# Half of the second MLP product of a decoder layer by seven block products for eight, its sums kept in SBUF

## The chip, the core and the metric

The kernel runs on one core of one Trainium2 chip. The metric is the device time of one execution in microseconds; three executions are shown. The engines of the core are TensorE (PE in the profile, with PEld for its weight loads), VectorE (DVE), ScalarE (ACT), GpSimd (POOL) and SyncE (SP). Each has a queue of its own, which it works off in order; waits between engines are semaphores.

## What is computed

One layer of a decoder on 256 tokens (16 meta tokens are put ahead of them), width 2048: a token-mixing half, then an MLP. The change lies in the MLP and the norm around it:

```python
h_res = h_res + merged @ w_out[l]
h2 = rms_norm(h_res, norm_mlp_g[l])
h_res = h_res + jnp.square(jax.nn.relu(h2 @ w_mlp_in[l])) @ w_mlp_out[l]
...
y = rms_norm(h_res, final_norm_g)
return y[:, N_META:N_META + S]
```

`w_mlp_in` is 2048 x 8192 and `w_mlp_out` 8192 x 2048, in float32. By the end of the token mixing the meta tokens have done their work, so the MLP has 256 token rows.

## The kernel before

**Numbers.** Every float32 operand is split into a high part that TensorE reads in one pass (fp32r) and a low rest. A product is three matmuls: high by high, high by low, low by high.

**The stream.** All weights go through one list of `blocks`. SP loads a unit of 1 MB into one of three `raw` buffers; a unit has two blocks of 128 x 1024 elements. `convert(i)` splits a block: ACT casts `raw` to `hi` (L228), DVE subtracts to get `lo` (L233). `hi` and `lo` have four buffers each, so ACT can start on block j only when PE has ended block j-4. The loop at L1123 does, for each block i: `convert(i + 3)`, then at most one small job from the `side` queue, then the block's matmuls. This text order is the order of every engine's queue.

**The MLP** (`mlp_group`, L919) goes through the 8192 hidden columns in four groups of 2048. In a group, four slabs of the first product (`slab_t`, L269, eight blocks each, 16 matmul pairs of 512 and 256 columns per unit) make 16 hidden chunks `hid` of 128 columns x 256 tokens. After a slab's last block a `wave` (L130) takes four PSUM banks out: per bank ACT copies one half, DVE adds the other, DVE squares the positive part (L932), ACT casts and DVE subtracts. Then four slabs of the second product (`slab_n`, L304), of 512 output columns each, use `hid` as stationary: a block is two chunks x two token halves x three matmuls (L319, L320, L321) = 12 matmuls of 128x512. After 16 chunks DVE adds each of the two banks to the residual, `hr += r2sq * ps` (L949). `r2sq` is the square of the norm's factor, which is taken out of the squared ReLU. The last slab of the last group is `slab_last`, whose two token halves end one after the other, with `final` behind each.

PSUM has eight banks: five of a pool `g` and three of a pool `m`. The MLP uses only `g`: four for a `slab_t`, two for a `slab_n`. GpSimd has nothing to do in the MLP.

Of the kernel before, what the change touches and what calls it, by code (L numbers as in the profile page):

```python
# [8 lines left out]
F32 = mybir.dt.float32  # L9
# [41 lines left out]
POOL_FROM, POOL_TO = 20, 112  # L51


class Slots:
    def __init__(self, pool, n, dtype, name):
        self.free = deque(pool.tile([P, 2, L], dtype, name=f"{name}{i}") for i in range(n))
        self.low = n
# [16 lines left out]
def decoder_layer(ctx, tc, x, meta, g_mix, w_in, kv_g, ik_g, w_uk, w_uv, w_ao, w_pool,  # L74
# [9 lines left out]
    ptp = ctx.enter_context(tc.tile_pool(name="ptp", bufs=2))  # L84
    evp = ctx.enter_context(tc.tile_pool(name="evp", bufs=1))
    stp = ctx.enter_context(tc.tile_pool(name="stp", bufs=4))
    pg = ctx.enter_context(tc.tile_pool(name="pg", bufs=5, space=PSUM))
# [4 lines left out]
    plain = Slots(act, NPLAIN, F32, "f")  # L92
# [49 lines left out]
    ident = cst.tile([P, P], F32, name="ident")  # L142
    dup = cst.tile([IDIM, P], F32, name="dup")
    ones = cst.tile([P, P], F32, name="ones")
# [13 lines left out]
    grow = cst.tile([KC, P], F32, name="grow")  # L158
    A.dma_start(out=grow, in_=gain_rows(g_mix))
    grow2 = cst.tile([27, P], F32, name="grow2")  # L160
# [14 lines left out]
    class Block:  # L175
        def __init__(self, unit, src, shape, mm, pops=1, pre=None):
            self.unit, self.src, self.shape, self.mm, self.pops, self.pre = unit, src, shape, mm, pops, pre
            self.split_late = self.keep = False

# [27 lines left out]
    def split_block(b, i):  # L207
# [9 lines left out]
        else:  # L217
# [16 lines left out]
            b.hi, b.lo = hv, lv  # L234

# [33 lines left out]
    def slab_t(w, c0, tiles, rhs, nk=KC, done=None, wide=None, lead=False):  # L269
        """Output tiles [128 columns of w, tokens]; weights stationary."""  # L270
# [3 lines left out]
        def mm(k):  # L274
            def go(hi, lo):
# [18 lines left out]
                if k + 2 == nk:  # L294
                    wave([done(j, pss[j]) for j in range(tiles)])
# [8 lines left out]
    def slab_n(w, k_base, c0, lhs, nk, done):  # L304
        """Output tiles [128 tokens, 512 columns of w]; activations stationary."""
# [26 lines left out]
    def slab_last(w, k_base, c0, lhs, nk, done):  # L332
        """As slab_n, but the second half of the tokens follows the first on the same, kept weights."""
# [109 lines left out]
    bias = cst.tile([P, SC], F32, name="bias")  # L443
# [422 lines left out]

    def reload_x():
        for s in range(4):
# [12 lines left out]
    def mean_sq(t=slice(0, 2)):  # L881
        V.tensor_reduce(ssum[:, t], ss[:, t], axis=AX.X, op=ALU.add)
        V.tensor_scalar(ssum[:, t], ssum[:, t], 1.0 / D, EPS, op0=ALU.mult, op1=ALU.add)
# [26 lines left out]

    def norm2_stat():
        mean_sq()
        V.reciprocal(r2sq, ssum)

# [1 line left out]
    def rhs_h2(k):  # L916
        return h2[k], 0

    def mlp_group(gi):  # L919
        hid = []  # L920

        def done_1(s):
            def go(j, ps):
                t = slots.get()
                hid.append(t)
                u, st = pair(ps)
# [7 lines left out]
            return go  # L934
# [4 lines left out]
        def done_2(s):  # L939
            def go(t, ps):  # L940
                f = flat(hr[t][s])[:, 0:512]

                def last():
                    if s == 3 and t == 1:
                        for m in hid:
                            slots.put(m)
                    if gi == 3:
                        push(lambda: final_pre(t, s))
                return [lambda: V.scalar_tensor_tensor(out=f, in0=ps, scalar=r2sq[:, t:t + 1], in1=f,  # L949
                                                       op0=ALU.mult, op1=ALU.add), last]  # L950
            return go

        for s in range(4):
            slab_t(w1, gi * D + s * 512, 4, rhs_h2, done=done_1(s))
# [8 lines left out]
    def load_gf():  # L963
# [5 lines left out]
        A.activation(rstd, ssum, AF.Sqrt)  # L969

    def final_pre(t, s):
        square_piece(t, s)
        f = flat(hr[t][s])[:, 0:512]
        V.tensor_tensor(out=f, in0=f, in1=flat(gf[s])[:, 0:512], op=ALU.mult)

    def final(t, ps):
        f = flat(hr[t][3])
# [189 lines left out]
```

## Time and profile before

| | us |
|---|---|
| three executions | 1422.92, 1422.93, 1424.09 |
| their median | 1422.93 |
| profiled execution, first to last instruction (its span) | 1421.2 |
| median less span | 1.7 |

The profile is of one execution. The page gives no other time for the profiled one than its span; the 1.7 us are start and end outside the first and last instruction. Busy times by engine within the span: PE 1409.1 us in 7748 matmuls, DVE 856.4, ACT 696.2, GpSimd 188.7. [...]

### The profile page before, as it was taken

Reading aid. Unit: us, or ns where it says so; the run is one execution under the profiler, and the core shown is the slowest. Engines: PE = TensorE matmul, PEld = TensorE weight load, DVE = VectorE, ACT = ScalarE, POOL = GpSimd, SP = SyncE. Lnnn points to the kernel's source line nnn. Section 1 sums busy time; section 2 is a strip of 40 time slices with the busy share of each in tenths; the row PEclk is TensorE's granted clock in tenths of the full one; section 3 lists DMA queues with packets and bytes.
Section 4 is the critical chain, followed back from the end, with each engine's and each line's share of the span. In section 5 each row is a group of like instructions: output and inputs, shape, how many; then the busy total and the mean of one; then the engine's idle time right before and its main releaser. Section 6 shows DMA issues by size and latency. Waiting matters only on the chain.

```text
span 1421.2 us, 19595 instructions
## 1 busy us (share of the span) xinstructions
PE 1409.1 (99%) x7748; PEld 1212.0 (85%) x7748; DVE 856.4 (60%) x1279; ACT 696.2 (49%) x1070; POOL 188.7 (13%) x145
## 2 busy tenths in 40 slices
PE   9999999999999999999999999999999999999997
PEld 8888888899988888888888888888888888888886
DVE  5667965565567767665566545566455654556654
ACT  5655465555555745444544433454334443445452
POOL 1155454454304000000000000000000000000000
PEclk9999999999999999999999999999999999999999
DMA  6654454434546565665555556555555555565552
GB/s 226 202 171 147 163 162 155 153 118 140 162 156 201 178 199 202 210 220 187 183 178 185 200 178 196 189 179 196 188 188 195 180 181 202 180 188 193 183 192 104
DMA packets 135723, 256.21 MB, mean 180 GB/s; under 512 B 4710, under 2 KB 16016, under 8 KB 135632
## 3 DMA queue, kind: packets, MB, share of 16 engines
q1 hardware_dynamic: 134352, 251.68, 53.2%
q0 software_dynamic: 1248, 3.29, 0.8%
q8 instruction: 60, 0.98, 0.3%
q14 instruction: 31, 0.25, 0.1%
q10 hardware_dynamic: 32, 0.01, 0.0%
HBM read 252.86 MB, written 2.10 MB: 179 GB/s over the span
## 4 chain that ended last, share of the span: by engine, by line
PE 94%; DVE 4%; ACT 1%; issue 0%; DMA 0%; POOL 0%; DVEq 0%; POOLq 0%; ACTq 0%
PE g L292 34%; PE g L293 17%; PE g L319 10%; PE g L321 10%; PE g L320 10%; PE g L137 2%; PE g L139 2%; PE g L138 2%; PE m L137 1%; DVE lo L231 1%; PE m L138 1%; PE m L139 1%; PE g L343 1%; PE g L341 1%; PE g L342 1%; DVE f L544 1%
## 5 line engine op out<-in xcount | busy, mean ns | idle before, releaser
L292 PE MATMUL g<-r,hi 128*128 128x512 f32 x2240 | 793.7, 396 | 1.0 <-DVE f L124 1.0
L228 ACT CAST hi<-raw 128x1024 fp32r<-128x1024 f32 (+1 forms) x469 | 486.8, 1046 | 566.2 <-PE g L292 269.5
L233 DVE TENSOR_TENSOR lo<-raw,hi 128x1024 fp32r<-128x1024 f32 (+1 forms) x377 | 457.7, 1224 | 410.2 <-ACT hi L228 409.4
L293 PE MATMUL g<-r,lo 128*128 128x256 f32 x2240 | 630.6, 282 | 0.0
L292 PEld LDWEIGHTS g<-r,hi 128*128 128x128 f32 x2240 | 420.8, 188 | 99.4 <-DVE f L124 2.1
L293 PEld LDWEIGHTS g<-r,lo 128*128 128x128 f32 x2240 | 423.2, 189 | 0.2
L319 PE MATMUL g<-hi,r 128*128 128x512 f32 x608 | 241.6, 397 | 0.0
L321 PE MATMUL g<-hi,r 128*128 128x512 f32 x608 | 238.7, 393 | 0.0
L320 PE MATMUL g<-lo,r 128*128 128x512 f32 x608 | 238.4, 392 | 0.0
L231 POOL TENSOR_TENSOR lo<-raw,hi 128x512 fp32r<-128x512 f32 x92 | 154.8, 1689 | 212.9 <-ACT hi L228 212.2
L321 PEld LDWEIGHTS g<-hi,r 128*128 128x128 f32 x608 | 114.1, 188 | 27.9
L231 DVE TENSOR_TENSOR lo<-raw,hi 128x512 fp32r<-128x512 f32 x92 | 83.1, 904 | 89.6 <-ACT hi L228 89.6
L320 PEld LDWEIGHTS g<-lo,r 128*128 128x128 f32 x608 | 114.2, 188 | 25.6
L319 PEld LDWEIGHTS g<-hi,r 128*128 128x128 f32 x608 | 114.1, 188 | 25.4
L123 ACT COPY b<-g 128x256 f32<-128x256 f32 x148 | 54.7, 371 | 25.0 <-PE g L293 21.2
L115 ACT CAST r<-t 128x256 fp32r<-128x256 f32 x100 | 40.7, 407 | 44.0 <-DVE t L932 27.7
L137 PE MATMUL g<-r,hi 128*128 128x272 f32 (+1 forms) x192 | 56.9, 297 | 0.0
L139 PE MATMUL g<-r,lo 128*128 128x272 f32 (+1 forms) x192 | 55.8, 291 | 0.0
L138 PE MATMUL g<-r,hi 128*128 128x272 f32 (+1 forms) x192 | 55.7, 290 | 0.0
L124 DVE TENSOR_TENSOR t<-g,b 128x256 f32<-128x256 f32 x116 | 48.0, 417 | 0.2 <-ACT b L123 0.2
L116 DVE TENSOR_TENSOR r<-t,r 128x256 fp32r<-128x256 f32 x100 | 42.8, 428 | 4.3 <-ACT r L115 0.2
L137 PEld LDWEIGHTS g<-r,hi 128*128 128x128 f32 x192 | 36.5, 190 | 0.8
(190 smaller groups left out, 921.0 us busy)
## 6 DMA issues: line engine op xcount, KB each, us to landing
raw<-in_w_mlp_in_dram SPq DMA_DIRECT2D x64, 1024.0 KB, 5.3
raw<-in_w_mlp_out_dram SPq DMA_DIRECT2D x64, 1024.0 KB, 5.1
raw<-in_w_in_dram SPq DMA_DIRECT2D x56, 1024.0 KB, 5.0
raw<-in_w_attn_o_dram SPq DMA_DIRECT2D x16, 1024.0 KB, 5.1
raw<-in_w_out_dram SPq DMA_DIRECT2D x16, 1024.0 KB, 5.1
raw<-in_w_pool_o_dram SPq DMA_DIRECT2D x8, 1024.0 KB, 5.1
raw<-in_w_in_dram SPq DMA_DIRECT2D x8, 512.0 KB, 7.9
raw<-in_w_in_dram SPq DMA_DIRECT2D x4, 768.0 KB, 5.1
```

Of the source, the lines that this page charges most:

```text
L123: return t, [lambda: A.copy(b, ps[:, 1]), lambda: V.tensor_tensor(out=t, in0=ps[:, 0], in1=b, op=ALU.add)]
L137: T.matmul(ps, wh, xh, start=first, stop=False)
L138: T.matmul(ps, wh, xl, start=False, stop=False)
L139: T.matmul(ps, wl, xh, start=False, stop=last)
L228: A.copy(hv, src)
L231: e.tensor_tensor(out=lv[:, kk], in0=src[:, kk], in1=hv.bitcast(F32)[:, kk], op=ALU.subtract)
L233: V.tensor_tensor(out=lv, in0=src, in1=hv.bitcast(F32), op=ALU.subtract)
L292: T.matmul(ps, wh, xt[:, :, o:o + S], start=f, stop=False)
L293: T.matmul(ps[:, 0], wl, xt[:, 0, o:o + S], start=False, stop=l)
L319: T.matmul(ps, xh, hi[:, kk], start=f, stop=False)
L320: T.matmul(ps, xh, lo[:, kk], start=False, stop=False)
L321: T.matmul(ps, xl, hi[:, kk], start=False, stop=l)
```

## The change

The second product of a group is now walked 1024 output columns at a time (`mix_group`, two walks n = 0 and 1 in groups 0 to 2, one in group 3). A walk has eight units; a unit p holds hidden chunks 2p and 2p+1 by 1024 columns, that is a 2 x 2 grid of weight pieces, against a 2 x 2 grid of hidden pieces (two chunks by two token halves). Units 0, 2, 4, 7 are done plainly: two blocks of 12 matmuls, eight products in all. Units 1, 3, 5, 6 (`SUMS`) are done by a scheme of seven products, in three blocks a, b, c of 6, 6 and 9 matmuls. Its operands are sums: of hidden pieces (`combs`, made once per group and unit in the waves of the first product) and of weight pieces (`sums_a`, `sums_b`, made on DVE for each unit before the blocks are split). Block c splits one more piece of 512 columns (`extra`).

The products of all units go into eight banks, all of PSUM: four of them (11, 12, 21, 22) take what belongs to one quarter of the output (128 tokens x 512 columns), the other four (1, 5, 6, 7) what several quarters share. At the end of a walk each bank is copied out by ACT (`drain`) into one of a few temporaries and added to a running sum in SBUF by a DMA with an add, issued by GpSimd (in group 0 the shared banks' sums are just begun by the copy). The running sums of the quarters are the residual itself, which is divided by `r2sq` first (`scale_up`) and multiplied by it at the end (`final_pre`, `final`). In the last walk of each column half the banks are added by DVE from PSUM (`f1`, `f2`, `out`), and the shared running sums are joined into the quarters by eight DVE adds out of the side queue (`join`). The second column half of group 3 stays with `slab_n` and `slab_last`. Some constants and buffers of the early stages now lie in pools that are closed before the MLP, so that its new tiles fit.

```diff
+NWORK = 20
+SUMS = (1, 3, 5, 6)
+WALK = ((0, 1, 2, 3, 4, 5, 6, 7), (1, 0, 3, 2, 5, 4, 6, 7))
...
+    def scale_up(t, s):
...
+        A.activation(flat(r)[:, 0:512], flat(r)[:, 0:512], AF.Copy, scale=msq[:, t:t + 1])
...
+        def sums_a():
...
+            V.tensor_tensor(out=two(tt["a"]), in0=two(raw[:, 512:1536]),
+                            in1=raw[:, 0:512].unsqueeze(1).to_broadcast([P, 2, 512]), op=ALU.add)
+
+        def sums_b():
...
+            V.tensor_tensor(out=tt["b"][:, 0:512], in0=tt["a"][:, 0:512], in1=raw[:, 1024:1536], op=ALU.add)
+            V.tensor_tensor(out=tt["b"][:, 512:1024], in0=tt["b"][:, 0:512], in1=raw[:, 1536:2048], op=ALU.add)
+
+        def extra():
...
+            A.copy(bc.hi2, raw[:, 1536:2048])
+            V.tensor_tensor(out=bc.lo2, in0=raw[:, 1536:2048], in1=bc.hi2.bitcast(F32), op=ALU.subtract)
...
+        def c_mm(p, kk, x):
+            def go(hi, lo):
+                for c in ("22", "21", "12", "11"):
+                    t, h = CROSS[c]
+                    mm_n(bank[c], *a(2 * p + kk, t), hi[:, h], lo[:, h], kk == 0 and x == (first_c if c == "22" else 0), x == 7 and kk == 1)
...
+            def go_a(hi, lo):
+                mm_n(bank["5"], *cb(1), hi[:, 0], lo[:, 0], fr, la)
+                mm_n(bank["7"], *cb(0), hi[:, 1], lo[:, 1], fr, la)
+
+            def go_b(hi, lo):
+                mm_n(bank["6"], *cb(2), hi[:, 0], lo[:, 0], fr, la)
+                mm_n(bank["21"], *a(kb, 1), hi[:, 1], lo[:, 1], x == 0, False)
+
+            def go_c(hi, lo):
+                mm_n(bank["1"], *a(ka, 0), hi[:, 0], lo[:, 0], fr, la)
+                mm_n(bank["12"], *cb(3), hi[:, 1], lo[:, 1], x == 0, False)
+                mm_n(bank["11"], *a(kb, 0), own[0].hi2, own[0].lo2, x == 0, False)
...
+        def drain(c):
+            first = gi == 0 and c not in CROSS
+            r = plain.get()
+            if first:
+                acc[n, c] = r
+            A.copy(flat(r)[:, 0:512], bank[c])
+            if not first:
+                d = flat(acc[n, c])[:, 0:512]
+                G.dma_start(out=d, in_=flat(r)[:, 0:512], accum_op=ALU.add)
+                plain.put(r)
...
+        if not final:
+            for i, c in ((ls + 2, "5"), (ls + 2, "7"), (ls + 3, "6"), (ls + 4, "1"), (e, "22"), (e, "21"),
+                         (e, "12"), (e, "11")):
+                at(i, drain, c)
...
+                return [lambda: None, lambda: None,
+                        lambda: tt(out=c4[:, 0:2], in0=u4[:, 1:2].to_broadcast([P, 2, P]), in1=u4[:, 0:4:3],
+                                   op=ALU.subtract),
+                        lambda: tt(out=c4[:, 2], in0=u4[:, 0], in1=c4[:, 1], op=ALU.subtract),
+                        lambda: tt(out=c4[:, 3], in0=u4[:, 2], in1=c4[:, 2], op=ALU.subtract)] + \
+                    split_stages(comb[p][0], cs[:, 0:S], S) + split_stages(comb[p][1], cs[:, S:2 * S], S)
...
-        for s in range(4):
-            if gi < 3 or s < 3:
-                slab_n(w2, gi * KC, s * 512, lhs_hid, KC, done_2(s))
-            else:
-                slab_last(w2, gi * KC, s * 512, lhs_hid, KC, final)
...
+        for n in range(2 if gi < 3 else 1):
+            mix_group(gi, n, hid, comb, bank)
+        at(len(blocks), free)
+        if gi == 3:
+            slab_n(w2, gi * KC, 1024, lhs_hid, KC, done_2(2))
+            slab_last(w2, gi * KC, 1536, lhs_hid, KC, final)
...
+        for fn in hooks.pop(i, ()):
+            fn()
+        if i + 4 < len(blocks) and blocks[i + 4].sums is not None:
+            blocks[i + 4].sums()
```

**Where it moves instructions.** DVE, from the end of the last wave of the first product into the second, in group 0. `lo` are the splits, `t` and `r` a hidden chunk before and after its split. Before:

```order
L932 SCALAR_TENSOR_TENSOR t<-t 128x256
L116 TENSOR_TENSOR r_98<-t,r_98 128x256
L116 TENSOR_TENSOR r_99<-t,r_99 128x256
L233 TENSOR_TENSOR lo<-raw,hi 128x1024 x8
L949 SCALAR_TENSOR_TENSOR f_135<-g,r2sq,f_135 128x512
```

Now (`cs` are sums of hidden pieces, `ta` and `tb` sums of weight pieces, `xl` the extra piece's low part):

```order
L1162 SCALAR_TENSOR_TENSOR t<-t 128x256
L123 TENSOR_TENSOR r_129<-t,r_129 128x256
L1173 TENSOR_TENSOR cs<-us 128x256
L123 TENSOR_TENSOR r_108<-t,r_108 128x256
L1175 TENSOR_TENSOR cs<-us,cs 128x128
L1176 TENSOR_TENSOR cs<-us,cs 128x128
L123 TENSOR_TENSOR r_109<-cs,r_109 128x256
L123 TENSOR_TENSOR r_116<-cs,r_116 128x256
L241 TENSOR_TENSOR lo<-tb,hi 128x1024
L241 TENSOR_TENSOR lo<-raw,hi 128x1024
L1000 TENSOR_TENSOR xl<-raw,xh 128x512
```

Five operations more stand between the wave and the first split behind it, and that split is now the one for block b of unit 1.

DVE further on, in the middle of the walk, units 4 to 6 (before, eight splits in a row and then two L949 stand here):

```order
L986 TENSOR_TENSOR ta<-raw 128x1024
L241 TENSOR_TENSOR lo<-raw,hi 128x1024
L992 TENSOR_TENSOR tb<-ta,raw 128x512
L993 TENSOR_TENSOR tb<-tb,raw 128x512
L241 TENSOR_TENSOR lo<-ta,hi 128x1024
L241 TENSOR_TENSOR lo<-tb,hi 128x1024
L986 TENSOR_TENSOR ta<-raw 128x1024
L241 TENSOR_TENSOR lo<-raw,hi 128x1024
L1000 TENSOR_TENSOR xl<-raw,xh 128x512
L992 TENSOR_TENSOR tb<-ta,raw 128x512
L993 TENSOR_TENSOR tb<-tb,raw 128x512
L241 TENSOR_TENSOR lo<-ta,hi 128x1024
```

The sums stand among the splits, one block ahead of the split that needs them.

ACT, from the last units of walk 0 into walk 1 (before, only casts `hi` stand here); `g` and `m` are the banks, `w` the temporaries and running sums:

```order
L1064 COPY w_6271<-g 128x512
L236 CAST hi<-ta 128x1024
L1064 COPY w_6272<-g 128x512
L236 CAST hi<-tb 128x1024
L1064 COPY w_6273<-g 128x512
L236 CAST hi<-raw 128x1024
L999 CAST xh<-raw 128x512
L1064 COPY w_6262<-g 128x512
L1064 COPY w_6263<-m 128x512
L1064 COPY w_6264<-m 128x512
L1064 COPY w_6265<-m 128x512
L236 CAST hi<-raw 128x1024 x2
```

The copies out of the banks stand among the casts of the next walk's first blocks; from group 1 on the four temporaries serve both for the first four copies and for the last four.

## Rows read from the trace of the kernel before

**Rows 1.** Page, parts 1 and 2: busy us by engine, then granted clock in tenths.
```profile
PE 1409.1 (99%) x7748; PEld 1212.0 (85%) x7748; DVE 856.4 (60%) x1279; ACT 696.2 (49%) x1070; POOL 188.7 (13%) x145
...
PEclk9999999999999999999999999999999999999999
```
**Rows 2.** Page, part 4: shares of the chain that ended last, by engine.
```profile
PE 94%; DVE 4%; ACT 1%; issue 0%; DMA 0%; POOL 0%; DVEq 0%; POOLq 0%; ACTq 0%
```
**Rows 3.** Waits, whole span: who waited for whom, us in total, times, longest.
```profile
PE g L292 <- DVE f L124: 1.0, 2, 0.5
...
DVE lo L233 <- ACT hi L228: 409.4, 311, 2.7
```
**Rows 4.** Page, part 5, second product: count, busy us, mean ns, idle before.
```profile
L319 PE MATMUL g<-hi,r 128*128 128x512 f32 x608 | 241.6, 397 | 0.0
```
**Rows 5.** Timeline of PE in a `slab_n`: start us, us, instruction.
```profile
979.88 0.39 PE L319 MATMUL g<-hi,r 128*128 128x512 f32 x1
980.11 0.39 PE L320 MATMUL g<-lo,r 128*128 128x512 f32 x1
...
983.34 0.39 PE L319 MATMUL g<-hi,r 128*128 128x512 f32 x1
```
**Rows 6.** Timeline of ACT in the same slab: casts of successive blocks, idle before.
```profile
975.22 1.05 ACT L228 CAST hi<-raw 128x1024 fp32r<-128x1024 f32 x1 [1.72 <-PE g L321]
977.99 1.05 ACT L228 CAST hi<-raw 128x1024 fp32r<-128x1024 f32 x1 [1.73 <-PE g L321]
```
**Rows 7.** Timeline of DVE: a single split, and six subtractions of 512 in a row.
```profile
1001.27 1.23 DVE L233 TENSOR_TENSOR lo<-raw,hi 128x1024 fp32r<-128x1024 f32 x1 [1.55 <-ACT hi L228]
...
1382.46 3.70 DVE L216 TENSOR_TENSOR r<-raw,r 128x512 fp32r<-128x512 f32 x6
```
**Rows 8.** Timeline of DVE, wave at the end of a first-product slab.
```profile
898.72 0.42 DVE L124 TENSOR_TENSOR t<-g,b 128x256 f32<-128x256 f32 x1
...
901.98 0.42 DVE L932 SCALAR_TENSOR_TENSOR t<-t 128x256 f32<-128x256 f32 x1
902.31 0.98 DVE L116 TENSOR_TENSOR r<-t,r 128x256 fp32r<-128x256 f32 x2
903.83 3.50 DVE L233 TENSOR_TENSOR lo<-raw,hi 128x1024 fp32r<-128x1024 f32 x3 [0.53 <-ACT hi L228]
```
**Rows 9.** Timeline of ACT, the same wave.
```profile
896.50 1.05 ACT L228 CAST hi<-raw 128x1024 fp32r<-128x1024 f32 x1 [1.75 <-PE g L292]
...
902.43 0.41 ACT L115 CAST r<-t 128x256 fp32r<-128x256 f32 x1 [0.59 <-DVE t L932]
902.75 2.00 ACT L228 CAST hi<-raw 128x1024 fp32r<-128x1024 f32 x2
904.94 1.06 ACT L228 CAST hi<-raw 128x1024 fp32r<-128x1024 f32 x1 [0.20 <-PE g L292]
```
**Rows 10.** Groups by line and shape: ACT operations of 512 columns.
```profile
L215 ACT CAST r<-raw 128x512 fp32r<-128x512 f32 x8 | 4.3, 616 | 0.0
```
**Rows 11.** DMA issues of the span: count, KB each, median us from issue to landing.
```profile
raw<-in_w_mlp_out_dram SPq DMA_DIRECT2D x64, 1024.0 KB, 5.1
...
f<-in_x_dram POOLq DMA_DIRECT2D x8, 256.0 KB, 3.5
...
f<-in_final_norm_g_dram POOLq DMA_DIRECT2D x4, 256.0 KB, 4.7
```
**Rows 12.** Line L871, GpSimd's loads of x: time to issue, time to landing.
```profile
L871 POOL DMA_DIRECT2D f<-in_x_dram x8: 538/538/585, 449.5 to 563.0; - x8
...
DMA to landing us min/median/max: 3.4/3.5/4.1
```
**Rows 13.** Groups by line and shape: DVE subtractions of 512, beside GpSimd's and alone.
```profile
L231 DVE TENSOR_TENSOR lo<-raw,hi 128x512 fp32r<-128x512 f32 x92 | 83.1, 904 | 89.6 <-ACT hi L228 89.6
...
L216 DVE TENSOR_TENSOR r<-raw,r 128x512 fp32r<-128x512 f32 x8 | 5.0, 686 | 0.0
```

More of the change, by code (lines that the diff above doesn't have):

```diff
@@ L1 @@
-from collections import deque
+from contextlib import ExitStack
+from collections import defaultdict, deque
 import concourse.bass as bass
@@ L91, in decoder_layer @@
     slots = Slots(act, NSLOT, F32R, "r")
-    plain = Slots(act, NPLAIN, F32, "f")
+    plain = Slots(fpl, NPLAIN, F32, "f")
     V, A, T, G = nc.vector, nc.scalar, nc.tensor, nc.gpsimd
@@ L178, in __init__ @@
             self.split_late = self.keep = False
+            self.sums = self.extra = None
     def add_unit(load, halves):
@@ L234, in split_block @@
             b.hi, b.lo = hv, lv
+            if b.extra is not None:
+                b.extra()
     side = deque()
@@ L294, in go @@
                 if k + 2 == nk:
-                    wave([done(j, pss[j]) for j in range(tiles)])
+                    jobs = [done(j, pss[j]) for j in range(tiles)]
+                    wave(jobs + (more() if more else []))
             return go
@@ L865, in decoder_layer @@
     h2 = [None] * KC
+    late = {}
     def reload_x():
+        nonlocal plain
+        early.close()
+        late["pool"] = ctx.enter_context(tc.tile_pool(name="late", bufs=1, reuse_waits="tile"))
+        plain = Slots(late["pool"], NWORK, F32, "w", S)
         for s in range(4):
@@ L916, in rhs_h2, with at, mm_n, sums_tile @@
     def rhs_h2(k):
         return h2[k], 0
+    hooks = defaultdict(list)
+    acc = {}
+    hc = hr
+    CROSS = {"11": (0, 1), "12": (0, 0), "21": (1, 1), "22": (1, 0)}
+    def at(i, fn, *args):
+        hooks[i].append(lambda: fn(*args))
+    def mm_n(ps, xh, xl, wh, wl, first, last):
+        T.matmul(ps, xh, wh, start=first, stop=False)
+        T.matmul(ps, xh, wl, start=False, stop=False)
+        T.matmul(ps, xl, wh, start=False, stop=last)
+    def sums_tile(tag):
+        return late["pool"].tile([P, 1024], F32, tag=tag, name=tag)
@@ new lines, in join, with v, done @@
+    def join(n):
+        def v(c):
+            return flat(acc[n, c])[:, 0:512]
+        for d, c, op in (("6", "1", ALU.subtract), ("7", "6", ALU.add), ("6", "5", ALU.add), ("5", "7", ALU.add),
+                         ("12", "6", ALU.add), ("21", "7", ALU.subtract), ("22", "5", ALU.add), ("11", "1", ALU.add)):
+            push(lambda d=d, c=c, op=op: V.tensor_tensor(out=v(d), in0=v(d), in1=v(c), op=op))
+        def done():
+            for c in ("6", "7", "5", "1"):
+                plain.put(acc.pop((n, c)))
+        push(done)
@@ L919, in mlp_group, with stages @@
     def mlp_group(gi):
         hid = []
+        comb = {}
+        us = {}
         def done_1(s):
-            def go(j, ps):
+            sp = [p for p in (2 * s, 2 * s + 1) if p in SUMS]
+            def stages(j, ps):
+                c = 4 * s + j
                 t = slots.get()
                 hid.append(t)
-                u, st = pair(ps)
+                dst = None
+                if c // 2 in sp:
+                    if c % 2 == 0:
+                        us[c // 2] = late["pool"].tile([P, 512], F32, tag="us", name="us")
+                    dst = us[c // 2][:, (c % 2) * S:(c % 2 + 1) * S]
+                u, st = pair(ps, dst)
@@ L940, in go, with free @@
             def go(t, ps):
[L941 to L950, printed above, removed]
-            return go
+                f = flat(hc[t][s])[:, 0:512]
+                return [lambda: V.tensor_tensor(out=f, in0=ps, in1=f, op=ALU.add),
+                        lambda: push(lambda: final_pre(t, s))]
+            return go
+        if gi in (2, 3):
+            at(len(blocks) + 3, join, 3 - gi)
         for s in range(4):
-            slab_t(w1, gi * D + s * 512, 4, rhs_h2, done=done_1(s))
-        for s in range(4):
-            if gi < 3 or s < 3:
-                slab_n(w2, gi * KC, s * 512, lhs_hid, KC, done_2(s))
-            else:
-                slab_last(w2, gi * KC, s * 512, lhs_hid, KC, final)
+            done, more = done_1(s)
+            slab_t(w1, gi * D + s * 512, 4, rhs_h2, done=done, more=more)
+        bank = {}
+        def free():
+            for m in [m for v in comb.values() for m in v] + (hid if gi < 3 else []):
+                slots.put(m)
+        for n in range(2 if gi < 3 else 1):
+            mix_group(gi, n, hid, comb, bank)
+        at(len(blocks), free)
+        if gi == 3:
+            slab_n(w2, gi * KC, 1024, lhs_hid, KC, done_2(2))
+            slab_last(w2, gi * KC, 1536, lhs_hid, KC, final)
     gf = []
```

172 lines of the change are left out of this document (143 added, 29 removed).

## The prediction

> **What bounds the kernel now.** The page's first part, the shares of the chain and the list of waits come first. PE is busy for 99% of the span at the full granted clock [rows 1], the chain that ended last is PE for 94% of it [rows 2], and PE waits almost nowhere: its longest entry for a matmul of the first product is 1.0 us in all, while DVE spends 409 us waiting for ACT's casts, which in turn wait for PE to free a buffer [rows 3]. So the time is PE's work, and time comes off if there are fewer matmuls and nobody else becomes late.
>
> What is one matmul worth? The list of costly groups gives 397 ns as its mean [rows 4], but the rows overlap. The timeline has two L319 fifteen starts apart at 979.88 and 983.34, so 3.46 / 15 = 0.231 us each; ACT's casts, each released by the end of a block of 12, come 2.77 us apart, again 0.231 [rows 5, 6]. I price by the pace. The Trainium skill (Trainium Kernel Development and Optimization, Performance Expectations) says the same against the busy rows: matmul busy time is a bad metric because matmuls are pipelined. By the row's length the 84 matmuls below would be worth 33 us; by the pace, which the trace shows, 19.4.
>
> **What goes on PE.** A walk replaces two `slab_n` of 96 matmuls by four plain units of 24 and four summed units of 21, 180 in all. Seven walks take away 7 x 12 = 84 matmuls of 128x512; each takes its own weight load with it. 84 x 0.231 = **19.4 us**.
>
> **What it adds on DVE, the engine to watch.** A split of 1024 costs 1.23 us alone, but three in a row take 3.50, so 1.167 each where DVE is pressed; six subtractions of 512 take 3.70, 0.617 each [rows 7, 8]. A plain unit is two splits, 2.33 us of DVE against 24 x 0.231 = 5.55 of PE. A summed unit is sum a (1.167), two sums b (1.234), three splits (3.50) and the extra piece (0.617): 6.52 us of DVE against 21 x 0.231 = 4.86 of PE. So DVE loses 1.7 us in each summed unit and gains it back in the plain ones: a walk is 35.4 us of DVE against 41.6 of PE. No row shows an add with a broadcast source; I price it as the subtraction of the same size.
>
> The tight place is walk 0, where DVE starts late. Call S the end of PE's last block of the first product; in the trace S is 899.3 (the cast at 904.94 starts at the end of a block, two blocks of 2.83 earlier is S) [rows 9]. The wave now ends at S + 4.0 (902.31 + 0.98) [rows 8]. Five DVE operations (256, 128, 128, 256, 256 columns, about 0.33 and 0.25 each by the spacing of the wave, 901.98 to 902.31) and two ACT casts of 0.41 come behind it in a chain, so ACT casts block b of unit 1 from about S + 4.9, and DVE splits it from S + 6.0 to 7.2. PE has 5.55 of unit 0 and 1.39 of block a until then, 6.94: late by **0.2 us, in each of four groups, 0.8 us**. From S + 6.0 DVE has no pause: rest of unit 1 three operations, 2.95 us, unit 2 2.33, unit 3 6.52, unit 4 2.33, unit 5 6.52, and block a of unit 6 with its sums 3.57. That is 24.2 us, so this split ends at S + 30.2. PE needs it after units 0 to 5, at 3 x 5.55 + 3 x 4.86 + 0.2 = S + 31.4. Slack 1.2 us, the smallest of the walk; without it DVE's lag would go to PE one for one. In walk 1 no two summed units are neighbours and DVE enters it with an empty queue: no wait.
>
> **ACT.** A walk adds four times 1.05 + 0.62 for the third block and the extra piece, and eight copies of a bank at about 0.6 (512 columns from SBUF take 0.616) [rows 10]: 23.4 + 4.8 = 28 of 41.6 us. Not full. What matters is what is queued behind a copy: the casts of the next blocks. In walk 0 of groups 1 and 2 the last copy (bank 11) goes into the temporary from which bank 1's DMA is still adding. By the order above bank 1's copy follows the cast of the next walk's block b: DVE goes on from S + 30.2 with the rest of unit 6, unit 7 and that block's sums, to S + 37.9, then the cast 1.05 and the copy 0.6, S + 39.6, 2.2 us before PE ends the walk at 41.6 + 0.2. Behind the last copy stand a cast (1.05) and a split (1.17) that PE needs 4.86 us into the next walk. So a landing is hidden up to 2.2 + 4.86 - 0.6 - 1.05 - 1.17 = 4.3 us. At the end of walk 1 of group 1 a slab of the first product follows with 8.5 us of prepared blocks: hidden up to 7.9.
>
> **The adding DMAs.** None is in the trace. The nearest rows are GpSimd's plain loads of the same 256 KB: 3.5 us (3.4 to 4.1), and 4.7 with a broadcast source [rows 11, 12]. An add reads its target as well; 1024 KB land in 5.1 us and 256 KB in 3.5, so another 256 KB is about 0.5. Lower bound 3.5, which costs nothing; upper bound twice the slow row, 9.4, which costs 2 x 5.1 + 1.5 = 11.7 us. I take 5.0, nearest to the loads: 2 x 0.7 = **1.4 us**. The Trainium skill (DMA: Bandwidth & Descriptors, Anatomy of one DMA) gives 2.0 us plus the bytes at 436 GB/s for this path; with the two source reads that Collectives: The Full Stack (The bandwidth ceiling) counts for an add, an estimate of 3.2 us for 512 KB. By it the term would be zero and the time 1.4 us less; the plain load's 3.5 is already longer, so I keep the rows.
>
> **At no cost.** The final adds of DVE (twice 12 of 512, 8 us) stand behind the walk's splits; the next slab's four banks are free first by two of them, at 4.4 us after unit 6, and PE needs the last one 7.7 after it; its third and fourth blocks need splits that are ready 3 and 2 us early. Without that cover each would cost 2 to 3 us. The eight `scale_up` (0.62 each) and the 16 `join` adds fall into first-product slabs, where ACT and DVE idle more than 1.5 us a block [rows 6, 7]. The unit loads stay 1 MB with 5.1 us to land; in the walk each is issued at least 6.5 us before its sum. The tail has the same operations in number and kind. SP and GpSimd carry nothing else.
>
> **Sum.** 1421.2 of span - 19.4 + 0.8 + 1.4 = 1404.0, plus the 1.7 us that the median of the runs, 1422.93, lies above the span: **1405.7 us**.
>
> **Rivals.** *DVE is somewhat longer than priced* (the broadcast source, a semaphore in each chain of sum, cast and split): the first 5% of the 24.2 us are covered by the slack, every further 1% costs 0.24 us a group. At 10% it is 4 x (2.4 - 1.2) = 4.9 us and nothing in walk 1 (38.9 of 41.6): 1410.6. For it: the slack is small, and single rows are 1.23, not 1.167 [rows 7]. Against: DVE's pressed rows keep one pace [rows 8].
>
> *DVE becomes the bound, and the kernel ends slower.* Beside GpSimd's subtractions DVE's 512 columns took 904 ns, alone 686, a factor of 1.32 [rows 13]. If GpSimd's adding DMAs or the broadcast stretched a walk's DVE work so, walk 0 would be late by 7.7 - 1.2 = 6.5 us and walk 1 by 46.7 - 41.6 = 5.1: 4 x 6.5 + 3 x 5.1 = 41 us, 1405.7 + 41 = 1447. It decides from a stretch of about 20%: 4 x 3.6 + 3 x 0.9 = 17 us, all that is gained. Against: GpSimd has only eight issues of 0.54 us in a walk, late in it [rows 12].
>
> *The adds land late*, at 9.4 us: 1405.7 + 10.3 = 1416.0. For it: they share the DMA engines with the weights. Against: so did the loads of x.
>
> *The change doesn't do what it says: the walks' matmuls lose the pace.* They jump among eight banks; 13.7 ns more on each of the 1260 would eat the 17.2 us that are left: 1423. Against: the first product goes around four banks without a gap [rows 3].
>
> **How the numbers follow.** Forecast (1403 to 1409) 0.58; DVE somewhat longer (1409 to 1420) 0.18; adds late (1409 to 1418) 0.13; pace lost 0.04; DVE the bound 0.07. 1402.5 to 1416 leaves out the last two and a fifth of the two before, 0.17. A measurement of this kernel can tell about 0.2%, 2.8 us. Faster 0.87, same 0.05, slower 0.08.
>
> **What would show it.** PE: 7664 matmuls, and starts 0.231 apart inside the walks (else the pace rival). Waits of PE on DVE `lo` in walk 0 of each group at block b of unit 1 and around unit 6: about 0.2 us a group and none; several us at every summed unit mean DVE is the bound, and the row of `ta` will say if it is the broadcast. ACT's copies waiting for a DMA in walk 0 of groups 1 and 2, and the adds' time to landing: 5 us or else. What would make the prediction wrong most easily is the length of the sums on DVE.

## The result and the profile after

The changed kernel takes 1411.03 us (median of four runs, 1408.33 to 1413.80), the kernel before 1423.47 beside it: ratio 0.9912, 95% interval 0.9898 to 0.9926. A later repeat gave 1411.43 and 0.9918 (0.9903 to 0.9933). So it is faster by 12.4 us (0.9%), and inside the range of 1402.5 to 1416; but the forecast case, 1403 to 1409, was missed by 2 us, and its 1405.7 by 5.3. The profiled execution has a span of 1409.7 us.

Page of the changed kernel: part 1 (busy us by engine, count), part 2 (granted clock), part 4 (shares of the chain that ended last).

```profile
PE 1391.6 (99%) x7664; PEld 1195.6 (85%) x7664; DVE 999.1 (71%) x1511; ACT 773.7 (55%) x1208; POOL 215.2 (15%) x177
...
PEclk9999999999999999999999999999999999999999
...
PE 75%; issue 12%; DVE 8%; DMA 3%; ACT 1%; POOL 1%; DVEq 0%; ACTq 0%; POOLq 0%
```

Against [rows 1, 2]: 84 matmuls fewer, as the diff says, and DVE's share up from 60 to 71% of a shorter span. The chain was PE and little else; now "issue", time in which an engine waited for nothing that the profile shows, is in it with 12%, and DVE and DMA with 11%. The waits of the whole span say where (who waited for whom, us in total, times, longest):

```profile
ACT w L1064 <- DMA w<-w: 11.7, 6, 3.6
DVE ta L986 <- DMA raw<-in_w_mlp_out_dram: 6.4, 3, 2.6
PE m L957 <- ACT w L1064: 2.4, 2, 1.6
PE g L958 <- DVE lo L241: 2.3, 5, 0.9
```

The DMA issues (count, KB each, median us from issue to landing), and then the adds' own line:

```profile
raw<-in_w_mlp_out_dram SPq DMA_DIRECT2D x64, 1024.0 KB, 5.3
...
w<-w POOLq DMA_DIRECT2D x32, 256.0 KB, 8.2
```
```profile
DMA to landing us min/median/max: 3.9/8.2/15.1
```

The adding DMAs (`w<-w`) land after 8.2 us in the median and up to 15.1, where 5.0 was priced between the plain loads' 3.5 and twice the slow row [rows 11, 12]. ACT's bank copies (L1064) wait for them, and PE for the copies.

One such landing is not the same as the next. The kernel issues the adds in bursts, and the first of each of the five bursts landed 3.9 to 6.4 us after its issue, near the 5.0; the later ones land one behind the other. The first four of group 1 were issued from 995.55 to 1000.39 and landed at 1000.16, 1003.04, 1005.87 and 1008.49; their times to landing are

```profile
DMA to landing us min/median/max: 4.6/7.5/8.1
```

So the long landings are those of adds that have others ahead of them.

For the places, PE's timeline was cut at the first matmul of each stage (us; the first product of a group, then its two walks; group 3 ends otherwise and is left out):

```
                 first g0  walks g0  first g1  walks g1  first g2  walks g2  first g3
before             90.73     88.76     89.99     88.78     89.99     89.18     89.92
changed            90.43     83.74     89.55     89.56     90.40     85.53     89.55
```

24 matmuls at 0.231 us are 5.5. The walks of group 0 gained 5.0; those of group 1 lost 0.8, those of group 2 gained only 3.7. The stretch in group 1 is the change from walk 0 to walk 1. ACT there (start us, us, instruction, in brackets its idle time and what ended it):

```profile
1001.46 0.59 ACT L1064 COPY w<-g 128x512 f32<-128x512 f32 x1
1003.14 0.59 ACT L1064 COPY w<-m 128x512 f32<-128x512 f32 x1 [1.09 <-DMA w<-w]
1005.97 0.59 ACT L1064 COPY w<-m 128x512 f32<-128x512 f32 x1 [2.24 <-DMA w<-w]
1008.59 0.59 ACT L1064 COPY w<-m 128x512 f32<-128x512 f32 x1 [2.03 <-DMA w<-w]
```

Each of the three waiting copies starts 0.1 us after one of the landings above. PE at the same time:

```profile
1005.42 0.40 PE L959 MATMUL g<-hi,r 128*128 128x512 f32 x1
1006.61 0.50 PE L957 MATMUL m<-hi,r 128*128 128x512 f32 x1 [0.80 <-ACT w L1064]
...
1007.18 0.40 PE L959 MATMUL m<-hi,r 128*128 128x512 f32 x1
1009.23 0.50 PE L957 MATMUL m<-xh,r 128*128 128x512 f32 x1 [1.65 <-ACT w L1064]
...
1010.18 0.49 PE L957 MATMUL g<-hi,r 128*128 128x512 f32 x1
1011.44 0.50 PE L958 MATMUL g<-lo,r 128*128 128x512 f32 x1 [0.77 <-DVE lo L241]
...
1013.00 0.63 PE L959 MATMUL m<-hi,r 128*128 128x512 f32 x1
1013.42 0.63 PE L957 MATMUL m<-hi,r 128*128 128x512 f32 x1
...
1015.42 0.40 PE L959 MATMUL m<-hi,r 128*128 128x512 f32 x1
```

Beyond the pitch of 0.231, the distance from start to start of successive matmuls (their rows overlap), the three gaps are 0.96, 1.82 and 1.03 us, 3.8 together. The first two are waits for the banks 12 and 11 themselves, the third for the split behind the last copy. Behind them the matmuls start 0.43 us apart (1013.00, 1013.42), and the windows (us, busy us by engine with counts, then granted clock, DMA share, GB/s) show why:

```profile
1011.00:1013.00 2.00, 1.56 (x5) 1.24 (x5) 2.00 (x3) 0.47 (x2) 0.00 (x0) 0.71 1.12 227
1013.00:1015.00 2.00, 2.00 (x6) 1.61 (x5) 1.97 (x4) 0.65 (x1) 0.00 (x0) 0.50 0.87 163
1015.00:1017.00 2.00, 2.00 (x9) 1.59 (x9) 1.94 (x2) 1.91 (x3) 0.00 (x0) 0.94 0.82 273
```

Behind the gaps the granted clock is 0.50, the 1.2 GHz level, from 1013 to 1015, and below 1.00 in the two windows beside it, which comes to some 3 us at that level. The ten matmuls from 1011.44 to 1015.42 take 3.98 us instead of 2.31, another 1.7. So of the 5.8 us that group 1's walks are longer than group 0's, 3.8 are waits and 1.7 clock. The span's mean, 9 in every slice, hides it.

The same happens once more at the end of walk 1 of group 1, in the first-product slab behind it. ACT and then PE:

```profile
1052.25 0.59 ACT L1064 COPY w<-m 128x512 f32<-128x512 f32 x1 [3.59 <-DMA w<-w]
...
1056.22 0.59 ACT L1064 COPY w<-m 128x512 f32<-128x512 f32 x1 [1.45 <-DMA w<-w]
1056.70 3.89 ACT L236 CAST hi<-raw 128x1024 fp32r<-128x1024 f32 x4
```
```profile
1059.06 0.39 PE L303 MATMUL g<-r,lo 128*128 128x256 f32 x1 [0.58 <-DVE lo L241]
```

The casts stand behind the last waiting copy, and the split that PE waits for behind the first cast. This is the 0.85 us by which the first product of group 2 is longer than that of group 1 (90.40 against 89.55).

In group 2 it looks different. ACT copies three banks in a row without waiting; DVE waits for weights instead:

```profile
1181.93 1.57 ACT L1064 COPY w<-m 128x512 f32<-128x512 f32 x3
...
1188.07 1.23 DVE L986 TENSOR_TENSOR ta<-raw 128x1024 f32<-128x1024 f32 x1 [2.36 <-DMA raw<-in_w_mlp_out_dram]
...
1199.69 1.23 DVE L986 TENSOR_TENSOR ta<-raw 128x1024 f32<-128x1024 f32 x1 [2.64 <-DMA raw<-in_w_mlp_out_dram]
```

The four weight loads issued from 1177 to 1196 landed after 8.5 to 10.8 us, where the median of all 56 loads of the walks is 5.3; in the run without adds, below, the five of that place took 5.2 to 8.6.

The code says why ACT is free in group 2: `join(1)`, at the start of group 2, returns four tiles to the pool (`NWORK` is 20: eight hold the residual and, until then, eight the shared sums), so eight temporaries are free in group 2 and four in group 1. The prediction had counted four in both.

### The profile page after: what moved, and what is told of

It reads as the page before. It is cut to its first block, busy times and chain, and to the rows that moved or that the text cites. A ratio compares the mean times of both kernels' runs of the same rounds, so it can differ in the third digit from the quotient of the medians.

```text
span 1409.7 us, 19906 instructions
## 1 busy us (share of the span) xinstructions
PE 1391.6 (99%) x7664; PEld 1195.6 (85%) x7664; DVE 999.1 (71%) x1511; ACT 773.7 (55%) x1208; POOL 215.2 (15%) x177
## 4 chain that ended last, share of the span: by engine, by line
PE 75%; issue 12%; DVE 8%; DMA 3%; ACT 1%; POOL 1%; DVEq 0%; ACTq 0%; POOLq 0%
PE g L302 29%; PE g L303 15%; PE g L332 3%; PE g L330 3%; PE g L331 3%; PE m L957 2%; PE m L959 2%; PE m L958 2%; DVE lo L241 2%; PE g L144 2%; PE g L146 2%; PE g L145 2%; PE m L144 1%; DMA raw<-in_w_mlp_out_dram 1%; DVE lo L239 1%
## 5 line engine op out<-in xcount | busy, mean ns | idle before, releaser
L236 ACT CAST hi<-raw 128x1024 fp32r<-128x1024 f32 (+1 forms) x441 | 455.1, 1045 | 370.1 <-PE g L302 232.1
L241 DVE TENSOR_TENSOR lo<-raw,hi 128x1024 fp32r<-128x1024 f32 (+1 forms) x349 | 422.9, 1222 | 245.2 <-ACT hi L236 244.2
L302 PEld LDWEIGHTS g<-r,hi 128*128 128x128 f32 x2240 | 420.9, 188 | 98.2 <-DVE f L131 2.1
L1067 POOL DMA_DIRECT2D w<-w x32 | 27.8, 1080 | 550.0 <-ACT w L1064 427.5
L957 PE MATMUL m<-hi,r 128*128 128x512 f32 x224 | 89.5, 400 | 0.8 <-ACT w L1064 0.8
L959 PE MATMUL m<-hi,r 128*128 128x512 f32 x224 | 88.6, 396 | 0.0
L958 PE MATMUL m<-lo,r 128*128 128x512 f32 x224 | 88.4, 395 | 0.0
L958 PE MATMUL g<-lo,r 128*128 128x512 f32 x168 | 66.4, 395 | 2.5 <-DVE lo L241 2.3
L957 PE MATMUL g<-hi,r 128*128 128x512 f32 x168 | 66.4, 395 | 0.0
L959 PE MATMUL g<-hi,r 128*128 128x512 f32 x168 | 66.4, 395 | 0.0
L330 PE MATMUL g<-hi,r 128*128 128x512 f32 x160 | 64.3, 402 | 0.0
L332 PE MATMUL g<-hi,r 128*128 128x512 f32 x160 | 63.3, 395 | 0.0
L331 PE MATMUL g<-lo,r 128*128 128x512 f32 x160 | 62.5, 390 | 0.0
L144 PE MATMUL g<-r,hi 128*128 128x272 f32 (+1 forms) x192 | 56.9, 296 | 0.0
L236 ACT CAST hi<-ta 128x1024 fp32r<-128x1024 f32 x28 | 29.4, 1051 | 47.8 <-DVE ta L986 29.2
## 6 DMA issues: line engine op xcount, KB each, us to landing
w<-w POOLq DMA_DIRECT2D x32, 256.0 KB, 8.2
```

Source lines behind the costliest of these rows:

```text
L144: T.matmul(ps, wh, xh, start=first, stop=False)
L236: A.copy(hv, src)
L241: V.tensor_tensor(out=lv, in0=src, in1=hv.bitcast(F32), op=ALU.subtract)
L302: T.matmul(ps, wh, xt[:, :, o:o + S], start=f, stop=False)
L330: T.matmul(ps, xh, hi[:, kk], start=f, stop=False)
L331: T.matmul(ps, xh, lo[:, kk], start=False, stop=False)
```

## The experiments

The theory after this profile: the missing gain went to the adding DMAs, (a) through copies that wait for a temporary still being added from, with the clock behind it, and (b) through weight loads that they slow. Rivals: DVE is the bound; the matmuls lose pace; each such DMA costs its share, whoever waits.

**No adds.** The bank is still copied, the DMA is gone.

```
-                d = flat(acc[n, c])[:, 0:512]
-                G.dma_start(out=d, in_=flat(r)[:, 0:512], accum_op=ALU.add)
```

> The changed kernel without its 32 adding DMAs: each bank is still copied by ACT into a temporary, and what the later groups should have added to the sums is left out, so the output is not the reference's. DVE, PE and ACT do what they did. My theory: the part of the gain that is missing (forecast 1405.7, measured 1411.0) went to the adding DMAs, through the four temporaries that come free late (8.2 us to landing, not 5.0), the weight loads beside them and the clock after the stall. Then about 1404.5 us: 1423 - 19.4 for PE's matmuls + 4 x 0.3 for the late block b of unit 1, and no ACT copy that waits for a DMA. Rival, DVE is the bound: its work is the same, so 1410 to 1411. Rival, the matmuls lose pace in the walks: 1410 to 1411 too, with starts more than 0.231 us apart inside the walks.

Measured: 1403.5 us (1403.19 to 1405.36), ratio 0.9863 (0.9849 to 0.9876). The walks of groups 0, 1 and 2 take 83.74, 83.73 and 83.79 us. The only gaps of PE over 0.25 us in all the walks are the four at block b of unit 1 in walk 0, 0.27 to 0.32 us. PE in its trace, at the start of group 0's walk 0, at that wait, and where it first reads the `lo` of block a of unit 6:

```profile
787.29 0.39 PE L957 MATMUL g<-hi,r 128*128 128x512 f32 x1
...
794.20 0.40 PE L957 MATMUL g<-hi,r 128*128 128x512 f32 x1
794.75 0.50 PE L958 MATMUL g<-lo,r 128*128 128x512 f32 x1 [0.16 <-DVE lo L241]
...
819.18 0.39 PE L958 MATMUL g<-lo,r 128*128 128x512 f32 x1
```

DVE there: the split of block b of unit 1, and that of block a of unit 6:

```profile
793.47 1.23 DVE L241 TENSOR_TENSOR lo<-tb,hi 128x1024 fp32r<-128x1024 f32 x1 [0.52 <-ACT hi L236]
...
816.61 1.22 DVE L241 TENSOR_TENSOR lo<-ta,hi 128x1024 fp32r<-128x1024 f32 x1
```

With S = 787.29, block b's split ends at S + 7.4 (forecast 7.2) and that of block a of unit 6 at 817.83, S + 30.5 (forecast 30.2), before PE asks for it at S + 31.9 (forecast 31.4). DVE is not the bound and the pace holds: both rivals fall. The adding DMAs cost 7.5 us.

**The same DMAs without adding.**

```
-                G.dma_start(out=d, in_=flat(r)[:, 0:512], accum_op=ALU.add)
+                G.dma_start(out=d, in_=flat(r)[:, 0:512])
```

> The changed kernel with the same 32 DMAs by the same queue and between the same tiles, but they overwrite instead of adding, so the output is not the reference's. Each moves 256 KB from one tile to another and doesn't read its target. If it is the transfer on chip as such that costs: as the changed kernel, 1410 to 1412, 8 us to landing. If it is the adding: landing near the plain loads' 3.5 to 5 us, at most one short wait of ACT in walk 0 of groups 1 and 2, and 1404.5 to 1407 us.

Measured: 1406.0 us (1405.47 to 1406.53), ratio 0.9877 (0.9864 to 0.9891). The time to landing of these DMAs:

```profile
DMA to landing us min/median/max: 2.5/5.5/8.8
```

The software queue's packets, MB and share of 16 engines, in this run:

```profile
q0 software_dynamic: 3808, 11.68, 2.3%
```

and in the changed kernel:

```profile
q0 software_dynamic: 5856, 11.68, 4.1%
```

Without any of the 32, that queue has 1248 packets and 0.8%. So an overwriting DMA is 80 packets and an adding one 144, and in engine time, summed over the 16 engines, (0.041 x 1409.7 - 0.008 x 1401.7) x 16 / 32 = 23.3 us for an add and, in the same way, 10.5 for a copy. Landings of 5.5 instead of 8.2 leave group 1's walks 1.8 us long instead of 5.8, and group 2's none. ACT still waits four times, 7.2 us in all and all in group 1, more than the one short wait that was expected. So of the 7.5 us some two thirds are the adding, and at most a third, 2.5 us, is the transfer: of that third 0.7 us stand ahead of the MLP and 0.5 at block b of unit 1 at the start of group 1, where no such DMA is near. That wait is 0.3 to 0.8 us in the runs that make each sum once, also in the hybrid below, which issues no such DMA in group 0.

**GpSimd adds in place of the DMA.**

```
-                G.dma_start(out=d, in_=flat(r)[:, 0:512], accum_op=ALU.add)
+                G.tensor_tensor(out=d, in0=d, in1=flat(r)[:, 0:512], op=ALU.add)
```

> The changed kernel with GpSimd adding each temporary into its running sum by an instruction of its own in place of the DMA; all is computed. GpSimd's add of 512 columns should take 1 to 2 us (its subtractions of the same size in the trace of before were of that order), so temporaries come free long before ACT wants them, and no DMA stands beside the weight loads. My theory: 1404.5 to 1407 us. Rival, GpSimd slows DVE while both read and write (904 ns for 686 in the rows of before): eight adds in a walk stretch some eight DVE operations by 0.22 us, 1.8 us a walk, hidden in walk 1; at most the same for walk 0 of groups 1 and 2, so 1406 to 1409. Rival, DVE is the bound already: 1411 or more.

Measured: 1415.16 us (1414.67 to 1416.37), ratio 0.9943 (0.9931 to 0.9955): slower than the changed kernel, and past what the theory and the first rival gave. Here DVE is the bound; of the 11.7 us over the run without adds, PE's waits for its splits are

```profile
PE g L958 <- DVE lo L241: 8.3, 11, 1.4
```

GpSimd in its group 1, five adds in a row:

```profile
1005.65 10.26 POOL L1067 TENSOR_TENSOR w<-w,w 128x512 f32<-128x512 f32 x5 [2.27 <-ACT w L1064]
```

and DVE meanwhile:

```profile
1008.51 1.79 DVE L1000 TENSOR_TENSOR xl<-raw,xh 128x512 fp32r<-128x512 f32 x1
1010.22 2.32 DVE L241 TENSOR_TENSOR lo<-raw,hi 128x1024 fp32r<-128x1024 f32 x1
1012.46 2.31 DVE L986 TENSOR_TENSOR ta<-raw 128x1024 f32<-128x1024 f32 x1
```

Beside a GpSimd add, a split that takes 1.22 us takes 2.32 and a subtraction of 512 takes 1.79 instead of 0.69: 1.1 us on each, not the factor of 1.32 of [rows 13]. DVE's busy time is 25 us longer than in the run without adds (998.8 to 1023.9) for 32 adds. The Trainium skill (SBUF — State Buffer, Who interferes with whom) says that a DVE instruction with two SBUF inputs contends with a GpSimd instruction that reads SBUF; the rows agree, with 1.1 us more for both lengths of DVE operation seen. The rival "DVE becomes the bound" was thus real, but for GpSimd's arithmetic, not for its DMAs: the changed kernel's `ta` takes 1.22 us like any other 1024.

**How much room DVE has.** No adds, and sum a of each summed unit done twice.

```
-            V.tensor_tensor(out=two(tt["a"]), in0=two(raw[:, 512:1536]), ...
+            for _ in range(2):
+                V.tensor_tensor(out=two(tt["a"]), in0=two(raw[:, 512:1536]), ...
```

> As the kernel without adding DMAs (their sums are left out), but DVE does the two-piece sum ahead of block a of each summed unit twice: 1.22 us more of DVE in each of 28 summed units, nothing more on PE. By the prediction's account DVE has 1.2 us to spare at block a of unit 6 in walk 0 and 6 us at the end of walk 1. Three or four of the doubled sums lie ahead of that place: 3.7 to 4.9 - 1.2 = 2.5 to 3.7 us in each of four groups, nothing in walk 1: 10 to 15 us over the kernel without adds, 1414 to 1420. Rival, DVE is the bound in every walk: 28 x 1.22 = 34 us more. Rival, DVE has several us to spare everywhere: no more than 2 us.

Measured: 1422.37 us (1420.57 to 1423.78), 18.9 over the kernel without adds, where 10 to 15 was expected and 34 by the rival. In walk 0 of group 0 PE waits 0.69 us at block b of unit 1 and then around unit 6:

```profile
819.77 0.50 PE L958 MATMUL g<-lo,r 128*128 128x512 f32 x1 [1.20 <-DVE lo L241]
...
822.84 0.51 PE L958 MATMUL g<-lo,r 128*128 128x512 f32 x1 [0.72 <-DVE lo L241]
...
835.93 0.50 PE L957 MATMUL m<-hi,r 128*128 128x512 f32 x1 [0.51 <-ACT w L1065]
842.64 0.50 PE L958 MATMUL g<-lo,r 128*128 128x512 f32 x1 [0.47 <-DVE lo L241]
```

Gaps of 1.36 at block c of unit 5 and 0.88 at block a of unit 6: with the first, less the usual 0.32, 2.6 us in walk 0, in the range of 2.5 to 3.7 and at the place that was named. What I had missed are the 0.68 and 0.64 at the change of walks: a DVE that leaves walk 0 late does not have walk 1's spare time yet. With what hangs on these gaps, walk 0 loses 3.0 us and walk 1, where there is one, 1.7. Group 1 loses another 1.4 by the clock: its gaps at unit 1 are 0.90 and 1.03, 1.3 us apart, and behind them the matmuls start 0.43 us apart:

```profile
976.00:978.00 2.00, 2.00 (x7) 0.58 0.07 16
```

That is 4 x 3.0 + 3 x 1.7 + 1.4 = 18.5 of the 18.9 us. The slack is confirmed: DVE's split for block a of unit 6 ends 4.15 us later against S than without the doubling (S + 34.7, with S = 788.10), and PE reads it 2.85 later (822.84), so 1.3 us were free; beyond it DVE's lag goes to PE.

**DVE adds the last four banks, DMAs the first four** (the hybrid).

```
             first = gi == 0 and c not in CROSS
+            if c in CROSS:
+                d = flat(acc[n, c])[:, 0:512]
+                V.tensor_tensor(out=d, in0=bank[c], in1=d, op=ALU.add)
+                return
             r = plain.get()
```

> The changed kernel with the adds of the last four banks of a walk (22, 21, 12, 11) made by DVE straight from the bank, and only the first four (5, 7, 6, 1) by copy and adding DMA; all is computed. 12 DMAs instead of 32, each temporary is used once in a walk, so ACT never waits for one. DVE gets 4 x 0.69 = 2.7 us at the end of walk 0 in groups 0, 1 and 2, and at the end of walk 1 in groups 0 and 1, where first-product work follows. My theory (the four temporaries and the mass of DMAs were the cost, and DVE has about 2 to 4 us to spare at the walk's end): 1404 to 1406. Rival, DVE has no room there: 3 x 2.7 us are lost, 1411. Rival, any adding DMA beside the weight loads costs its share (12 of 32 of the 7.5 us): 1406 to 1407.

Measured: 1404.51 us (1403.88 to 1404.64), ratio 0.9864 (0.9848 to 0.9881). All is computed, and it beats both kernels: 6.5 us under the changed one, 1.0 over the one without adds. Both rivals (1411, 1406 to 1407) fall. Its 12 adds land hardly sooner (7.7 us), but no copy waits. Walks: 83.73, 84.08, 83.80, and the 0.35 in group 1 stand at its start, ahead of its adds. In the same window where the changed kernel's clock fell:

```profile
1010.00:1015.00 5.00, 5.00 (x24) 1.00 0.55 195
```

**DVE adds all eight.** The same with `if not first:` as its condition.

> The changed kernel with all 32 adds made by DVE straight from the bank: no temporary, no ACT copy and no DMA for them; all is computed. DVE gets 8 x 0.69 = 5.5 us at the end of walk 0 in groups 1 and 2, 2.7 in group 0. Where the doubled sum left DVE 2.3 us late at the end of a walk, PE waited 1.3 us there, so about 1 us of such a delay was free. If that is the room: 2 x 4.5 + 1.7 = 10.7 us, 1414. If DVE has 4 us, as a landing was priced (hidden up to 4.3): 2 x 1.2 = 2.4 us, 1406. If DVE's work in walk 1 has the 6 us to spare that the sum says and PE's queue of prepared blocks covers them: 1404.

Measured: 1407.5 us (1407.04 to 1408.02), ratio 0.9886 (0.9872 to 0.9901), near the case of 4 us of room. An add from a bank takes DVE 0.68 us. Walks: 83.74, 85.66, 85.74. The loss is one wait at the change of walks in each of groups 1 and 2, for a bank that DVE empties late (the second at 1182.35 is its twin):

```profile
1007.09 0.50 PE L957 MATMUL m<-hi,r 128*128 128x512 f32 x1 [1.68 <-DVE w L1063]
```

**Adds of the first four banks only.** The last four are copied and dropped.

```
+            if c in CROSS:
+                plain.put(r)
-            if not first:
+            elif not first:
```

> The changed kernel with the adding DMAs of the first four banks of a walk alone (12 of them); the last four are copied by ACT and their sums are left out. No copy of ACT ever waits for a landing, but the adds still share the DMA engines with the weight loads. If the wait for temporaries is the cost: as without any add, 1403 to 1404.5. If the cost is what adds do to the loads beside them: 12 / 32 of 7.5 us at least, 1406 or more, with DVE waiting for raw.

Measured: 1411.15 us (1410.43 to 1412.12), ratio 0.9912 (0.9898 to 0.9927). The edit did not do what I said of it: the temporaries go round in a queue, so the last four copies still take the tiles from which the first four are being added, and ACT waits as before:

```profile
ACT w L1064 <- DMA w<-w: 10.8, 6, 2.3
```

Read so, it is the sharpest of the runs. It has the hybrid's 12 DMAs, with the same landing of 7.7 us, and the whole loss of the changed kernel, all of it in group 1 (walks 83.73, 91.14, 84.17). The hybrid differs in that DVE empties the last four banks and they need no temporary: 6.6 us. ACT's four copies as such cost nothing: the run without adds has them too, and no waits. What group 2 gains by the adds that are gone (84.17 for 85.53), group 1 loses by a stall that is longer (91.14 for 89.56), with a clock of 0.72 still from 1015 to 1020 where the changed kernel's, whose group 1 starts 1.2 us sooner, was back at 0.98.

**The changed kernel again**, unchanged, beside these three.

> The changed kernel once more beside the others, on the same chip: 1408 to 1414 us, median near 1411, with ACT waiting for adding DMAs in the walks of groups 1 and 2.

Measured: 1411.43 us (1410.24 to 1415.05), walks 83.74, 90.29, 85.41. ACT waits for adds six times, as before, but all of it in group 1 and none in group 2.

**DVE adds the last four in group 1 alone.** The hybrid with `if gi == 1 and c in CROSS:`; 24 adding DMAs stay.

> The changed kernel with one difference: in group 1 alone, where only four temporaries are free, DVE adds the last four banks of each walk straight from the bank. 24 of the 32 adding DMAs stay, all 16 of groups 0 and 2 among them; all is computed. My theory: what costs is that in group 1 the last four copies wait for the landing of the first four; in group 2, where eight temporaries are free, nothing of ACT waits, and only the weight loads are slowed (1.7 us there in the changed kernel). So 1405 to 1406.5, with the stage of group 1 back at about 84 us from 89.6 and that of group 2 still at 85.5. Rival, each adding DMA costs its share of the 7.5 us by loading the DMA engines: 24 / 32, so 1409.

Measured: 1406.54 us (1405.47 to 1406.68), ratio 0.9879 (0.9864 to 0.9894), at the upper end of the theory's 1405 to 1406.5. Walks 83.75, 83.74, 85.64: group 1 is whole again, group 2 as before. ACT waits for no add at all. What is left in group 2 is (b), and its entries of the waits are

```profile
DVE ta L986 <- DMA raw<-in_w_mlp_out_dram: 7.2, 5, 2.7
...
PE g L958 <- DVE lo L241: 1.6, 4, 1.0
```

The rival by which each DMA costs its share would have been 1409. It falls.

**The hybrid turned round**, DVE the first four and DMAs the last four, `if not first and c not in CROSS:`.

> The hybrid turned round: DVE adds the first four banks of a walk (5, 7, 6, 1) straight from the bank, the last four (22, 21, 12, 11) go by copy and adding DMA; all is computed. 20 DMAs, and no copy meets a temporary whose add hasn't landed by long. My theory: no waiting copy, so 1404 to 1406, with what the four late adds in each of groups 1 and 2 do to the weight loads (up to 0.9 each). Rival, each DMA costs its share: 20 / 32 of 7.5 us, 1408. Rival, DVE has no room ahead of the walk's last splits: 2.7 us in groups 1 and 2 are lost, 1409.

Measured: 1406.38 us (1405.09 to 1406.96), ratio 0.9877 (0.9861 to 0.9894), just over what was expected. Walks 83.73, 84.43, 85.09: no copy waits, but four adds issued at the walk's end meet the next walk's loads, and in group 2 one `ta` waits 3.9 us for `raw`. Both rivals (1408, 1409) fall. Which four go by DMA matters a little; that the early ones have landed before those loads count is argued, not tried by itself.

## Why the prediction came out as it did

**PE's 19.4 us and the 0.8** held, the total in part by luck. Without adds the span is 1401.7, 19.5 under before, and 18.6 was forecast. Each group's two walks gained 5.0 to 5.4 against 5.54 - 0.2, and the stage from group 3's walk to the end 2.1 against 2.6: 17.6 in all, 1.0 less than forecast. The first-product stages, which had no term, are 1.5 us shorter together, and 0.4 lie ahead of the MLP. Block b of unit 1 is late in all four groups, by 0.3 and not 0.2.

**DVE's account** held: 1.22 us for the broadcast sum, the slack at block a of unit 6 about 1.3 where 1.2 was said. Both DVE rivals were wrong for this kernel, and the run with the doubled sum shows how near they were: 2.6 us lost in walk 0 for three more sums, 3.7 us, of DVE ahead of that block.

**The step that failed is the term of the adding DMAs**, 1.4 us, measured 7.5. Three parts of it:

- The landing, 5.0 from the nearest loads, is 8.2. The estimate "another 256 KB is about 0.5" took an add for a longer load; it is 144 packets for 80 and 2.2 times the engine time. And it priced one add by itself, which the first of a burst bears out (3.9 to 6.4); the fourth of group 1, bank 1's, on which that sum hung, landed after 8.1 behind three others. The trace of before has loads of the same size among others, at the start of the kernel (`f<-in_x_dram SPq DMA_DIRECT2D x8, 256.0 KB, 7.9`), and not only the 3.5 of [rows 11]. The 3.2 us estimated from the Trainium skill (DMA: Bandwidth & Descriptors, Anatomy of one DMA) does not agree either: the fastest of 32 landed in 3.9. An upper bound of 9.4 was the nearer end, and the rival made from it, "the adds land late" (1409 to 1418), is the case that came.
- Who waits. By the prediction only the last copy, in groups 1 and 2, beyond 4.3 us. In walk 0 of group 1 three copies waited (1.09, 2.24, 2.03 us), for 3.8 us of PE, which is what that working gives at 8.1 (8.1 - 4.3 = 3.8), though PE stood still for two banks first, and these the working had left out. At the end of walk 1, where a landing was to be hidden up to 7.9, three more waited, for 0.85 us of PE in the profiled run and none in the repeat. In group 2 none did: eight temporaries, not four. The share that the sum gave to group 2 rested on a miscount.
- What follows, which had no term. PE's stall was followed by matmuls at the 1.2 GHz level, which cost 1.7 us more, and adds slow the weight loads: 1.7 us in group 2, through `ta` waiting for `raw`. The prediction put the loads at no cost, with 5.1 us to land and 6.5 before their sums; they took up to 10.8. "They share the DMA engines with the weights" stood there as an argument for late adds, and not for late weights.

5.8 + 1.7 + 0.85 = 8.4 us by stages agrees with the 8.0 between the two spans (in the changed kernel's the stretch ahead of the MLP is 0.45 us shorter). That (a) and not (b) is the larger part is shown by the hybrid against the run with the first four adds only, and by the run that changes group 1 alone. More temporaries in group 1 were not tried; group 2, with eight, is the nearest to it. What the clock adds beyond the wait was read off the rows and not tried by itself.

The changed kernel's times spread more (1408.3 to 1415.1 in eight runs) than the hybrid's (0.8 us); the stall and the clock behind it are the likely source, but this is only argued.

## What to carry to other kernels

A DMA on chip that takes over an engine's work must be priced by its landing beside the traffic that is there and behind those issued just before it, and by the number of tiles it holds meanwhile: count the free temporaries at each place, stage by stage. Where a queue of copies goes round through few temporaries, splitting the work (half by the DMA, half by an engine that has a microsecond or two to spare there) removed the wait here at almost no cost. Look for small stalls of PE in the windows with their clock, since the time after the stall counts too.

## What was not expected of the hardware

- Adding DMAs from tile to tile of 256 KB: 8.2 us to landing (3.9 to 15.1) beside weight loads and one behind the other, overwriting ones 5.5 (2.5 to 8.8). GpSimd's part of issuing one is 0.86 us in the median for an add and 0.54 for an overwrite. While adds run, the DMA engines are busy at low throughput: share 1.01 to 1.08 at 213 to 288 GB/s in group 1 of the changed kernel, 0.91 to 0.94 at 350 with overwriting ones.
- GpSimd's addition of 512 columns cost DVE 1.1 us in each of the three operations shown, 25 us in all for 32 additions.
- Three gaps in PE's work in a row (0.96, 1.82 and 1.03 us, the changed kernel) were followed by some 3 us at the 1.2 GHz level, and so were two of 0.90 and 1.03 (group 1 with the doubled sum, clock 0.58); a single gap of 1.84 (the run in which DVE adds all eight) and the two of 1.36 and 0.88 (group 0 with the doubled sum) were not: the clock stays at 1.00 there.
